# The odd layer's S5 and MLA half rewritten: regrouping through DRAM, scans in pieces, the mask as four extra contraction rows, weight loads issued ahead

## The chip, the cores and the metric

The kernel runs on one core of a Trainium2 chip. The metric is device time in microseconds (us), the median of several executions. Engines are named as the profile names them: PE is TensorE (matmul), DVE is VectorE, ACT is ScalarE, POOL is GpSimd, SP is SyncE, which here only issues DMAs.

## The reference, cut to what matters

A trunk of two residual layers over x (1, 512, 1024) in float32. Layer 0 (even) is Mamba-2 beside differential attention; layer 1 (odd) is an S5 complex-diagonal SSM beside multi-head latent attention (MLA). Each mixer is followed by a SwiGLU. The change lies in the odd mixer:

```python
u, c_q, c_kv, k_rope = split_cols(h @ w_in, ODD_SIZES)      # 512, 384, 256, 32 columns
# S5: 32 groups of 16 channels, a complex state of 64 per group
bu = einsum('bsgh,gph->bsgp', ug, b_bar)
state = associative_scan(s5_combine, (a_el, bu), axis=1)
y = real(einsum('bsgp,ghp->bsgh', state, cm)) + d_skip * ug
y = gelu(y);  y_c = y * sigmoid(y @ w_glu + b_glu)
# MLA, 8 heads, key chunk of 64 <= query chunk of 64
q = rms_norm(c_q, q_norm) @ w_uq;  kv = rms_norm(c_kv, kv_norm) @ w_ukv
p = softmax(where(mask, (qn @ kn.T + qr @ k_rot.T) * scale, -inf));  y_d = p @ v
out = concatenate([y_c, y_d]) @ w_out
```

## The kernel before, in words

Activations stand feature-major, as 128 x 512 tiles (features on partitions, time on columns). A projection is a list of **units**. A unit is one output block of 128 columns; it is computed by `mm3` (L178 to L180) in three passes per k-tile, high by high, low by high and high by low, because weights and activations are split into two float32r halves. 24 matmuls of 128 x 512 make a unit with eight k-tiles. `prep` loads a chunk of weights (`wload`, L157, two buffers `raw`) and splits one unit of it: ACT casts the high half (`whi`, L169), DVE subtracts the low half (`wlo`, L170). There are two buffers of each half, two PSUM buffers `mm` for the results of units, and two each of `sc`, `tp` and `po`.

`drive` walks one hand-written list of units and closures, and prepares the next unit ahead of computing one. `later(n, f)` puts a closure off by n units. A scheduler then keeps each engine's instructions nearly in that order; every engine works through its own queue in order, and waits on semaphores.

In the odd layer the list is: four units of u; two of ck (256 columns of the latent key and value); three of cq (384 of the latent query); kr (32 rotary key columns); then the value product, the first query and key units of MLA, the GLU, the attention. Four S5 steps Q = 0 to 3 (128 channels each) lie between the units:

- `ev_u` scales u and regroups it into `u4[Q]` with 16 copies of 32 x 128, half on DVE and half on ACT (L1262).
- `s5a` makes 8 products u by b of 128 columns in two `sc` buffers (L1273), turns them by four multiplies on DVE (L1281 to L1284) and two sums on POOL, scans with eight `tensor_tensor_scan` (L1289), and turns back (L1299 to L1304) into `hr` and `hi`.
- `s5b`, two units later, makes 12 products (L1312 to L1315), adds the skip (L1320), takes the GELU on ACT, and regroups into `yf[Q]` with 16 more copies (L1326).

`ev_c` reads a unit of ck or cq out of its `mm` buffer three times: ACT high half, DVE low half (L344), ACT square (L273, L276). POOL sums the squares (L281), and `rows_k` and `rows_q` make the norms from a small PE product of that sum (L309) and a chain of 4-column DVE instructions. `attend`, `flip` and `scores` run the MLA heads in 16 steps (four pairs of heads by four query blocks). A score (L1412) is a product over 96 rows (64 plain and 32 rotary) in plain float32; a bfloat16 product of one row (L1414, `mrow` by `nrow`) adds -1e30 on the last 64 keys for the first 64 queries. The second head's probabilities are scaled on POOL (L1420).

Of the kernel before, what the change touches and what calls it, by code (L numbers as in the profile page):

```python
# [14 lines left out]
ALU = mybir.AluOpType  # L15
# [106 lines left out]
class Trunk:  # L122
# [81 lines left out]

# [39 lines left out]
    def drive(self, items):  # L244
        us = [x for x in items if isinstance(x, dict)]
        nxt = {id(u): v for u, v in zip(us, us[1:])}
        self.prep(us[0])
        for x in items:
            if isinstance(x, dict):
                if id(x) in nxt:  # L250
                    self.prep(nxt[id(x)])
                self.compute(x)
            else:
                x()
# [14 lines left out]
    def stat_add(self, st, src, pool=None, tag="sacc"):  # L269
# [4 lines left out]
        else:  # L274
            sq = self.t(self.tmp, [P, T], "sq")
            nc.scalar.activation(out=sq, in_=src, func=AF.Square)  # L276
            self.padd(st["acc"], st["acc"], sq)

# [91 lines left out]
    def setup(self):  # L370
# [12 lines left out]
        self.raws, self.kept = {}, {}  # L383
# [848 lines left out]
    def odd(self, E):  # L1232
# [7 lines left out]
        def start():  # L1240
            nonlocal sp
            sp = self.pool(ctx, "od")
            self.norm_done(E)
# [11 lines left out]
        def ev_u(Q, ps):  # L1255
# [4 lines left out]
            for q in range(4):  # L1260
                for i in range(4):
                    (A.copy if i % 2 else V.tensor_copy)(out=u4[Q][32 * i:32 * i + 32, q, :],  # L1262
                                                         in_=us[32 * q:32 * q + 32, i * P:(i + 1) * P])
# [4 lines left out]
        def s5a(Q):  # L1268
            S = self.s5
            pb = [self.ps("sc") for _ in range(2)]  # L1270
# [15 lines left out]
            self.padd(t[2], t[2], t[3], ALU.subtract)  # L1286
            for q in range(4):
# [4 lines left out]
            c_, s_ = (S[n][Q].rearrange("p q c -> p (q c)") for n in ("rc", "rs"))  # L1292
            if Q % 2:
                hr, hi = (t5(f"b{ri}{Q // 2}").rearrange("p (q c) -> p q c", q=4) for ri in range(2))
# [10 lines left out]
            self.later(2, lambda: s5b(Q, hr, hi))  # L1305

        def s5b(Q, hr, hi):
            S = self.s5
# [15 lines left out]
            for j in range(4):  # L1324
                for q in range(4):
                    (A.copy if q % 2 else V.tensor_copy)(out=yf[Q][32 * q:32 * q + 32, j * P:(j + 1) * P],  # L1326
                                                         in_=yy[32 * j:32 * j + 32, q * P:(q + 1) * P])
# [62 lines left out]
        def ev_qk(m, n):  # L1390
            def f_(ps):
                if n == 0:
                    qk[m] = [None, None]
                x = qk[m][n] = [t5(f"{('b1', 'rc')[n]}{2 * (m % 2) + hh}") for hh in range(2)]
# [11 lines left out]
        def scores(m, qb):  # L1406
# [3 lines left out]
            for hh in range(2):  # L1410
                ps = self.ps("sc")
                PE.matmul(ps[:, :n], lhsT=qk[m][0][hh][0:96, qb * P:(qb + 1) * P], rhs=qk[m][1][hh][0:96, :n],  # L1412
                          start=True, stop=False)
                PE.matmul(ps[:, n - 64:n], lhsT=self.mrow, rhs=self.nrow, start=False, stop=True)  # L1414
# [4 lines left out]
            for hh, e in enumerate((V, G)):  # L1419
                e.tensor_scalar(out=pp[hh][:, :n], in0=pp[hh][:, :n], scalar1=rr[:, hh:hh + 1], scalar2=None,  # L1420
                                op0=ALU.mult)
# [218 lines left out]
```

## Time and profile before

| what | value |
|---|---|
| median of 3 runs | 1457.12 us (1453.04 to 1458.03) |
| the profiled execution | 1457.81 us |
| its span, first to last instruction | 1456.0 us |
| PE busy over the span | 1395.0 us (96%) |
| DVE, ACT, POOL busy | 950.5, 674.0, 257.3 us |
| mean granted PE clock | 0.985 |

The span is what the trace covers; 1.8 us of the execution lie outside it. A busy share is the time in which an engine had an instruction running. The odd layer's first unit ends near 839 us of the span and its last near 1084.

### The profile page before, as it was taken

Reading aid. Unit: us, or ns where it says so; the run is one execution under the profiler, and the core shown is the slowest. Engines: PE = TensorE matmul, PEld = TensorE weight load, DVE = VectorE, ACT = ScalarE, POOL = GpSimd, SP = SyncE. Lnnn points to the kernel's source line nnn. Section 1 sums busy time; section 2 is a strip of 40 time slices with the busy share of each in tenths; the row PEclk is TensorE's granted clock in tenths of the full one; section 3 lists DMA queues with packets and bytes.
Section 4 is the critical chain, followed back from the end, with each engine's and each line's share of the span. In section 5 each row is a group of like instructions: output and inputs, shape, how many; then the busy total and the mean of one; then the engine's idle time right before and its main releaser. Section 6 shows DMA issues by size and latency. Waiting matters only on the chain.

```text
span 1456.0 us, 18392 instructions
## 1 busy us (share of the span) xinstructions
PE 1395.0 (96%) x6979; PEld 1142.9 (78%) x6979; DVE 950.5 (65%) x1992; ACT 674.0 (46%) x1222; POOL 257.3 (18%) x208
## 2 busy tenths in 40 slices
PE   8999989999999999999999987789999999999997
PEld 5877878888888777888888876666788888888887
DVE  6988788878766998773644589676664433433453
ACT  6658777867643443333232443365453322322342
POOL 0234511000012110010011313413121100100111
PEclk9999999999999999999999998889999999999999
DMA  5211121222213222222323211110222322223231
GB/s 183 81 72 59 59 87 44 73 73 73 88 58 116 75 90 104 96 88 83 112 88 104 89 55 36 54 47 1 87 87 93 111 87 95 105 80 111 87 102 59
DMA packets 20280, 119.83 MB, mean 82 GB/s; under 512 B 2384, under 2 KB 3024, under 8 KB 9056
## 3 DMA queue, kind: packets, MB, share of 16 engines
q1 hardware_dynamic: 18896, 116.89, 23.2%
q10 hardware_dynamic: 1296, 1.76, 0.4%
q8 instruction: 55, 0.90, 0.3%
q14 instruction: 33, 0.27, 0.1%
HBM read 116.55 MB, written 2.10 MB: 81 GB/s over the span
## 4 chain that ended last, share of the span: by engine, by line
PE 69%; DVE 20%; ACT 6%; issue 2%; POOL 2%; DMA 1%; SPq 0%; ACTq 0%; DVEq 0%; POOLq 0%
PE mm L178 13%; PE mm L179 13%; PE mm L180 13%; PE sc L180 7%; PE sc L179 7%; PE sc L178 7%; DVE wlo L170 3%; DVE qsw L608 2%; ACT qsw L768 1%; PE sc L1412 1%; ACT whi L169 1%; POOL xs L281 1%; PE po L1440 1%; PE po L857 1%; PE tp L1430 1%
## 5 line engine op out<-in xcount | busy, mean ns | idle before, releaser
L169 ACT CAST whi<-raw 128x1024 fp32r<-128x1024 f32 (+5 forms) x231 | 224.1, 970 | 537.9 <-PE mm L179 306.8
L170 DVE TENSOR_TENSOR wlo<-raw,whi 128x1024 fp32r<-128x1024 f32 (+5 forms) x231 | 264.9, 1147 | 43.8 <-ACT whi L169 28.9
L281 POOL TENSOR_TENSOR gt<-gt,rbc 128x512 f32<-128x512 f32 x44 | 76.3, 1736 | 572.7 <-ACT gt L967 572.7
L972 DVE TENSOR_TENSOR gt<-mm,gt 128x512 f32<-128x512 f32 x44 | 30.4, 690 | 110.9 <-PE mm L180 107.5
L281 POOL TENSOR_TENSOR sacc<-sacc,sq 128x512 f32<-128x512 f32 x29 | 45.2, 1558 | 262.8 <-issue 193.9
L966 DVE TENSOR_TENSOR gt<-sc,rbc 128x512 f32<-128x512 f32 x44 | 30.3, 689 | 89.1 <-PE sc L180 89.1
L180 PE MATMUL mm<-x0h,wlo 128*128 128x512 f32 (+2 forms) x91 | 36.9, 406 | 12.8 <-DVE wlo L170 12.8
L178 PE MATMUL mm<-x0h,whi 128*128 128x512 f32 (+2 forms) x91 | 38.9, 428 | 8.2 <-ACT x0h L343 6.0
L987 DVE TENSOR_TENSOR h<-h,mm 128x512 f32<-128x512 f32 x20 | 13.7, 687 | 44.0 <-PE mm L180 44.0
L768 ACT ACTIVATE qsw<-mm 32x512 f32<-32x512 f32 x64 | 37.7, 590 | 6.5 <-DVE qraw L764 5.7
L987 DVE TENSOR_TENSOR h<-h,sc 128x512 f32<-128x512 f32 x20 | 13.7, 686 | 38.8 <-PE sc L180 38.8
L967 ACT ACTIVATE gt<-gt 128x512 f32<-128x512 f32 x44 | 27.6, 628 | 22.9 <-DVE gt L966 22.9
L180 PE MATMUL mm<-x1h,wlo 128*128 128x512 f32 (+2 forms) x91 | 37.2, 409 | 0.0
L179 PE MATMUL mm<-x2l,whi 128*128 128x512 f32 (+2 forms) x91 | 37.1, 407 | 0.0
L178 PE MATMUL mm<-x7h,whi 128*128 128x512 f32 (+2 forms) x95 | 37.1, 390 | 0.0
L180 PE MATMUL mm<-x7h,wlo 128*128 128x512 f32 (+2 forms) x95 | 37.1, 390 | 0.0
L179 PE MATMUL mm<-x7l,whi 128*128 128x512 f32 (+2 forms) x95 | 37.0, 389 | 0.0
L178 PE MATMUL mm<-x1h,whi 128*128 128x512 f32 (+2 forms) x91 | 36.5, 401 | 0.3 <-ACT x1h L343 0.3
L179 PE MATMUL mm<-x0l,whi 128*128 128x512 f32 (+2 forms) x91 | 36.6, 402 | 0.2 <-DVE x0l L344 0.2
L178 PE MATMUL mm<-x2h,whi 128*128 128x512 f32 (+2 forms) x91 | 36.7, 404 | 0.0
L180 PE MATMUL mm<-x2h,wlo 128*128 128x512 f32 (+2 forms) x91 | 36.7, 403 | 0.0
L179 PE MATMUL mm<-x1l,whi 128*128 128x512 f32 (+2 forms) x91 | 36.4, 400 | 0.2 <-DVE x1l L344 0.2
(939 smaller groups left out, 4366.3 us busy)
## 6 DMA issues: line engine op xcount, KB each, us to landing
raw<-in_f_dram SPq DMA_DIRECT2D x52, 1024.0 KB, 4.8
raw<-in_w_dram SPq DMA_DIRECT2D x35, 1024.0 KB, 4.9
raw<-in_f_dram SPq DMA_DIRECT2D x16, 896.0 KB, 4.5
raw<-in_w_dram SPq DMA_DIRECT2D x8, 512.0 KB, 3.6
h<-in_xt_dram SPq DMA_DIRECT2D x8, 256.0 KB, 5.9
raw<-in_w_dram SPq DMA_DIRECT2D x2, 640.0 KB, 4.0
out_dram<-otm SPq DMA_DIRECT2D x4, 256.0 KB, 2.5
out_dram<-otm ACTq DMA_DIRECT2D x4, 256.0 KB, 2.8
```

The source lines that it names most:

```text
L169: nc.scalar.copy(out=hi[:, :n], in_=raw[:, o:o + n])
L170: nc.vector.tensor_tensor(out=lo[:, :n], in0=raw[:, o:o + n], in1=hi[:, :n].bitcast(F32), op=ALU.subtract)
L178: nc.tensor.matmul(ps, lhsT=hi[:, k, :m], rhs=xh, start=start and j == 0, stop=False)
L179: nc.tensor.matmul(ps, lhsT=hi[:, k, :m], rhs=xl, start=False, stop=False)
L180: nc.tensor.matmul(ps, lhsT=lo[:, k, :m], rhs=xh, start=False, stop=stop and j == n - 1)
L281: self.nc.gpsimd.tensor_tensor(out=out, in0=x, in1=y, op=op)
L608: V.scalar_tensor_tensor(out=acc, in0=xr[:, 1 + k:1 + k + T], scalar=self.par("cw", 12 * k + j), in1=acc, op0=ALU.mult, op1=ALU.add)
L768: A.activation(out=sw[c * 32:(c + 1) * 32, :], in_=ps[d * 32:(d + 1) * 32, :], func=AF.Identity, scale=scale)
L966: V.tensor_tensor(out=gt, in0=ps, in1=E["rbc"], op=ALU.mult)
L967: A.activation(out=gt, in_=gt, func=AF.Silu)
L972: V.tensor_tensor(out=gt, in0=ps, in1=gt, op=ALU.mult)
L987: V.tensor_tensor(out=self.h[i], in0=self.h[i], in1=ps, op=ALU.add)
```

## The change

- **Regrouping.** `regroup` replaces the 32 copies of an S5 step (16 for u4, 16 for yf): one DMA writes the 128 x 512 tile to DRAM, four DMAs read it back, 32 partitions each, all issued on SP.
- **Pieces.** `s5a` and `s5b` become one generator with three `yield`s; the list calls the pieces at chosen places. The products go to `po` buffers instead of `sc`.
- **Mask.** Four rows of the input `cmask` are loaded by DMA (issued on ACT) into rows 96 to 99 of the query and key tiles, eight DMAs of 4 x 512. A score is one product over 100 rows; the 32 one-row products go. Head pairs 2 and 3 use the tiles of pairs 0 and 1 again.
- **Scaling.** The second head's probabilities are scaled on ACT instead of POOL.
- **Loads.** `fetch` issues the next chunk's weight DMA as soon as fewer than two loaded chunks still have units to split. On SP this only changes what stands ahead of what: the load before the other DMAs.

```diff
+    def fetch(self):
+        for k in self.order:
+            if k not in self.raws:
+                if sum(self.left[x] > 0 for x in self.raws) >= 2:
+                    return
+                self.raws[k] = self.wload(k)
...
+    def regroup(self, out, src):
+        d = self.t(self.dram, [P, T], "regroup", bufs=4)
+        self.nc.sync.dma_start(out=d, in_=src)
+        for i in range(4):
+            self.nc.sync.dma_start(out=out[32 * i:32 * i + 32],
+                                   in_=d.rearrange("(q p) (i c) -> p i q c", q=4, i=4)[:, i])
...
-            for q in range(4):
-                for i in range(4):
-                    (A.copy if i % 2 else V.tensor_copy)(out=u4[Q][32 * i:32 * i + 32, q, :],
-                                                         in_=us[32 * q:32 * q + 32, i * P:(i + 1) * P])
+            self.regroup(u4[Q], us)
...
-            pb = [self.ps("sc") for _ in range(2)]
+            pb = [self.ps("po") for _ in range(2)]
...
-            self.later(2, lambda: s5b(Q, hr, hi))
-
-        def s5b(Q, hr, hi):
-            S = self.s5
+            yield
...
-                x = qk[m][n] = [t5(f"{('b1', 'rc')[n]}{2 * (m % 2) + hh}") for hh in range(2)]
+                if m < 2:
+                    x = [t5(f"{('b1', 'rc')[n]}{2 * (m % 2) + hh}") for hh in range(2)]
+                    for hh in range(2):
+                        A.dma_start(out=x[hh][96:100, :], in_=a["cmask"][4 * n:4 * n + 4, :])
+                else:
+                    x = qk[m - 2][n]
+                qk[m][n] = x
...
-                PE.matmul(ps[:, :n], lhsT=qk[m][0][hh][0:96, qb * P:(qb + 1) * P], rhs=qk[m][1][hh][0:96, :n],
-                          start=True, stop=False)
-                PE.matmul(ps[:, n - 64:n], lhsT=self.mrow, rhs=self.nrow, start=False, stop=True)
+                PE.matmul(ps[:, :n], lhsT=qk[m][0][hh][0:100, qb * P:(qb + 1) * P],
+                          rhs=qk[m][1][hh][0:100, :n], start=True, stop=True)
...
-            for hh, e in enumerate((V, G)):
-                e.tensor_scalar(out=pp[hh][:, :n], in0=pp[hh][:, :n], scalar1=rr[:, hh:hh + 1], scalar2=None,
-                                op0=ALU.mult)
+            V.tensor_scalar(out=pp[0][:, :n], in0=pp[0][:, :n], scalar1=rr[:, 0:1], scalar2=None, op0=ALU.mult)
+            A.mul(out=pp[1][:, :n], in_=pp[1][:, :n], mul=rr[:, 1:2])
...
-        items = [start] + uu
-        items += [L(s5a, 0), uck[0], L(s5a, 1), uck[1], lambda: self.later(1, rows_k, rows_k2), ucq[0], L(s5a, 2),
-                  ucq[1], ucq[2], L(s5a, 3), lambda: self.later(1, rows_q, rows_q2)] + ukr
-        items += [uv, uqr(0)] + uqk(0) + uqk(1) + [uqr(1)]
+        items = [start] + uu[:3] + [s5(0), uu[3], s5(0), uck[0], s5(1, 0), uck[1], lambda: self.later(1, rows_k, rows_k2),
+                                    s5(1), ucq[0], s5(1), s5(0), ucq[1], s5(2), ucq[2], s5(2, 1),
+                                    lambda: self.later(1, rows_q, rows_q2)]
+        items += ukr + [s5(3, 2), uv, s5(3, 2), uqr(0), s5(3)] + uqk(0) + [s5(3)] + uqk(1) + [uqr(1)]
```

What the order of instructions becomes, at three places.

**The first S5 step, DVE and PE.** DVE before, from the copies of the last u unit on (t and hr, hi belong to step Q = 0; raw_7825 holds the weights of ck, and wlo_7914 is the low half of ck's second unit):

```order
L1262 COPY u_1457_7858<-us_7856 32x128 x8
L1281 TENSOR_TENSOR t_1460_7885<-sc_7875,rc_1134_5482 128x512
L1282 TENSOR_TENSOR t_1461_7886<-sc_7876,rs_1135_5483 128x512
L1283 TENSOR_TENSOR t_1462_7887<-sc_7876,rc_1134_5482 128x512
L1284 TENSOR_TENSOR t_1463_7888<-sc_7875,rs_1135_5483 128x512
L1289 SCALAR_TENSOR_TENSOR t_1460_7885<-s5r_1065_4973,t_1460_7885 128x128 x4
L1289 SCALAR_TENSOR_TENSOR t_1462_7887<-s5r_1065_4973,t_1462_7887 128x128 x4
L1299 TENSOR_TENSOR hr_7903<-t_1460_7885,rc_1134_5482 128x4x127
L1301 TENSOR_TENSOR hi_7904<-t_1462_7887,rc_1134_5482 128x4x127
L1303 TENSOR_TENSOR hr_7903<-hr_7903,t_1461_7886 128x4x127
L170 TENSOR_TENSOR wlo_7914<-raw_7825,whi_7913 128x1024
L344 SCALAR_TENSOR_TENSOR ck0l_7943<-mm_7917,par_94,ck0h_7942 128x512
```

DVE now, at the same place (wlo_7868 is the low half of ck's second unit, wlo_7935 that of cq's first):

```order
L170 TENSOR_TENSOR wlo_7868<-raw_7658,whi_7867 128x1024
L1304 TENSOR_TENSOR t_1459_7811<-po_7801,rc_1135_5484 128x512
L1307 TENSOR_TENSOR t_1462_7814<-po_7801,rs_1136_5485 128x512
L1305 TENSOR_TENSOR t_1460_7812<-po_7802,rs_1136_5485 128x512
L1306 TENSOR_TENSOR t_1461_7813<-po_7802,rc_1135_5484 128x512
L1313 SCALAR_TENSOR_TENSOR t_1459_7811<-s5r_1066_4975,t_1459_7811 128x128 x4
L1313 SCALAR_TENSOR_TENSOR t_1461_7813<-s5r_1066_4975,t_1461_7813 128x128 x4
L1325 TENSOR_TENSOR hr_7924<-t_1459_7811,rc_1135_5484 128x4x127
L1327 TENSOR_TENSOR hi_7925<-t_1461_7813,rc_1135_5484 128x4x127
L1329 TENSOR_TENSOR hr_7924<-hr_7924,t_1460_7812 128x4x127
L170 TENSOR_TENSOR wlo_7935<-raw_7765,whi_7934 128x1024
L368 SCALAR_TENSOR_TENSOR ck0l_7899<-mm_7873,par_94,ck0h_7898 128x512
```

The copies are gone, and each split has moved up by one unit: ck's second stands ahead of step 0 and cq's first behind it. PE before, from the end of step 0's second products (mm_8064 is cq's first unit, sc_8095 step 1's second products, tp_8131 the sum of ck's squares):

```order
L1315 MATMUL sc_8024<-hi_7904,cx_1097_5157 128x128
L178 MATMUL mm_8064<-x0h_7393,whi_7988 128x512
...
L180 MATMUL mm_8064<-x7h_7638,wlo_7989 128x512
L1312 MATMUL sc_8095<-u_1446_7760,tt_1160_5723 128x128
...
L309 MATMUL tp_8131<-ones_97,sacc_7946 128x1 x4
L1273 MATMUL sc_8156<-u_1451_7808,b_1193_6033 128x128 x4
```

PE now (mm_7938 is ck's second unit, mm_7984 cq's first, mm_8080 cq's second; sc_8050 is step 0's second products):

```order
L180 MATMUL mm_7938<-x7h_7640,wlo_7868 128x512
L178 MATMUL mm_7984<-x0h_7397,whi_7934 128x512
...
L180 MATMUL mm_7984<-x7h_7640,wlo_7935 128x512
L333 MATMUL tp_8015<-ones_97,sacc_7902 128x1 x4
L1335 MATMUL sc_8050<-u_1445_7745,tt_1124_5397 128x128
...
L178 MATMUL mm_8080<-x0h_7397,whi_7978 128x512
```

The sum of ck's squares (tp) now stands ahead of step 0's second products, which stood one unit before it.

**SP, from the last u units on.** Before, these are weight loads alone. Now (regroup is the DRAM tile, us the scaled u or the S5 output, u the regrouped u4, and raw_8194 of before is raw_7871 here):

```order
L157 DMA raw_7765<-in_w_dram 128x2048
L298 DMA regroup_7746<-us_7743 128x512
L298 DMA regroup_7755<-us_7752 128x512
L300 DMA u_1445_7745<-regroup_7746 32x4x128 x4
L300 DMA u_1448_7754<-regroup_7755 32x4x128 x4
L298 DMA regroup_7795<-us_7792 128x512
L298 DMA regroup_7853<-us_7850 128x512
L157 DMA raw_7871<-in_w_dram 128x1280
L300 DMA u_1455_7794<-regroup_7795 32x4x128 x4
L300 DMA u_1467_7852<-regroup_7853 32x4x128 x4
L157 DMA raw_7982<-in_w_dram 128x1408
L298 DMA regroup_8070<-us_8063 128x512
```

Two writes stand ahead of the reads of the first, and one weight load stands between the third and fourth write and their reads.

**ACT, where the GLU meets the first attention steps.** Before, the sigmoid of the last GLU unit and the exponentials of the first scores (us is the sigmoid's output, rs the probabilities):

```order
L1457 ACTIVATE us_8725<-mm_8712,par_94 128x512
L1416 ACT_TABLE_LOAD
L1416 ACTIVATE rs_1639_8735,ssum_8733<-sc_8737,nmx_8732 128x512
L1462 CAST t_1634_8728<-us_8725 128x512
L1416 ACTIVATE rs_1640_8736,ssum_8733<-sc_8742,nmx_8732 128x512
L169 CAST whi_8925<-raw_8923 128x512
```

Now, from the third GLU unit's sigmoid on:

```order
L1481 ACTIVATE us_8633<-mm_8620,par_94 128x512
L1441 ACT_TABLE_LOAD
L1441 ACTIVATE rs_1655_8683,ssum_8681<-sc_8685,nmx_8680 128x384
L1486 CAST t_1637_8636<-us_8633 128x512
L1481 ACT_TABLE_LOAD
L1481 ACTIVATE us_8657<-mm_8644,par_94 128x512
L1441 ACT_TABLE_LOAD
L1441 ACTIVATE rs_1656_8684,ssum_8681<-sc_8689,nmx_8680 128x384
L1486 CAST t_1643_8660<-us_8657 128x512
```

Sigmoids and exponentials alternate now. Over the whole program ACT loads a function table 31 times instead of 28; all three are in this stretch.

## Rows read from the trace of the kernel before

**Rows 1.** Windows: length, busy us of PE, PEld, DVE, ACT, POOL, PE clock, DMA.

```profile
860.00:885.00 25.00, 16.35 (x84) 13.50 (x82) 24.59 (x33) 4.33 (x7) 14.16 (x14) 0.86 0.09 27
885.00:910.00 25.00, 19.69 (x103) 16.83 (x104) 21.84 (x58) 11.11 (x25) 7.17 (x6) 0.86 0.08 29
910.00:942.00 32.00, 25.35 (x130) 19.47 (x129) 24.31 (x53) 11.87 (x24) 16.57 (x10) 0.93 0.18 60
942.00:962.00 20.00, 15.67 (x63) 13.15 (x64) 13.29 (x29) 10.43 (x24) 2.63 (x2) 0.69 0.00 1
1000.00:1057.00 57.00, 57.00 (x338) 39.30 (x337) 33.03 (x76) 25.62 (x68) 13.11 (x11) 1.00 0.16 56
```

**Rows 2.** PE's waits between 830 and 1090: total us, times, longest.

```profile
PE mm L180 <- DVE wlo L170: 12.2, 3, 6.1
PE tp L326 <- DVE rkr L319: 4.8, 1, 4.8
PE sc L1312 <- ACT b L1379: 4.4, 1, 4.4
PE mm L178 <- DVE b L1397: 3.5, 1, 3.5
```

**Rows 3.** Timeline of DVE in the S5 stretch: start, us, instruction.

```profile
847.03 1.06 DVE L1257 TENSOR_TENSOR us<-sc,rbc 128x512 f32<-128x512 f32 x1
...
870.11 2.27 DVE L170 TENSOR_TENSOR wlo<-raw,whi 128x1024 fp32r<-128x1024 f32 x1
872.30 0.74 DVE L344 SCALAR_TENSOR_TENSOR ck0l<-mm,par,ck0h 128x512 fp32r<-128x512 f32 x1
...
885.39 0.74 DVE L344 SCALAR_TENSOR_TENSOR ck1l<-mm,par,ck1h 128x512 fp32r<-128x512 f32 x1
```

**Rows 4.** Timeline of ACT, 870 to 980.

```profile
873.13 0.60 ACT L273 ACTIVATE sacc<-mm 128x512 f32<-128x512 f32 x1 [7.60 <-DVE ck0l L344]
...
886.16 0.60 ACT L276 ACTIVATE sq<-mm 128x512 f32<-128x512 f32 x1 [5.32 <-DVE ck1l L344]
...
968.21 1.28 ACT L1457 ACT_TABLE_LOAD   x1
969.51 0.69 ACT L1457 ACTIVATE us<-mm,par 128x512 f32<-128x512 f32 x1
```

**Rows 5.** Timeline of POOL, the sum of ck's squares.

```profile
886.83 1.28 POOL L281 TENSOR_TENSOR sacc<-sacc,sq 128x512 f32<-128x512 f32 x1 [2.37 <-ACT sq L276]
```

**Rows 6.** Timeline of PE: ck's second unit, then scores without and with the mask product.

```profile
865.59 0.48 PE L178 MATMUL mm<-x0h,whi 128*128 128x512 f32 x1
...
961.95 1.02 PE L1412 MATMUL sc<-rc,b 96*128 96x512 f32 x2
...
963.04 0.40 PE L179 MATMUL mm<-cq0l,whi 128*128 128x512 f32 x1
963.27 0.39 PE L180 MATMUL mm<-cq0h,wlo 128*128 128x512 f32 x1
...
991.69 1.12 PE L1412 MATMUL sc<-rc,b 96*128 96x512 f32 x2
992.74 0.20 PE L1414 MATMUL sc<-nrow,mrow 1*128 1x64 bf16 x1
992.87 1.12 PE L1412 MATMUL sc<-rc,b 96*128 96x512 f32 x2
```

**Rows 7.** Groups of instructions, 836 to 1060: count, busy us, mean ns.

```profile
L1416 ACT ACTIVATE rs<-sc,nmx 128x512 f32<-128x512 f32 (+3 forms) x32 | 16.9, 528 | 16.2 <-DVE nmx L1415 14.8 <-DVE rsum L1418 1.0
...
L1326 DVE COPY yf<-us 32x128 f32<-32x128 f32 x32 | 7.9, 248 | 0.4
```

**Rows 8.** Page, DMA issues: count, KB each, median us from issue to landing.

```profile
raw<-in_w_dram SPq DMA_DIRECT2D x35, 1024.0 KB, 4.9
...
h<-in_xt_dram SPq DMA_DIRECT2D x8, 256.0 KB, 5.9
...
out_dram<-otm SPq DMA_DIRECT2D x4, 256.0 KB, 2.5
```

**Rows 9.** The line of the weight loads between 836 and 1090: ns to issue one.

```profile
L157 SPq DMA_DIRECT2D raw<-in_w_dram x10: 327/328/328, 847.1 to 1047.6; - x10
```

More of the change, by code (lines that the diff above doesn't have):

```diff
@@ L200, in prep @@
         o = sum(CH[u["key"]][2][:u["sub"]])
+        self.left[u["key"]] -= 1
         u["w"] = self.wsplit(self.raws[u["key"]], o, u["nk"], u["m"], u["keep"])
@@ L246, in drive @@
         nxt = {id(u): v for u, v in zip(us, us[1:])}
+        seen = set()
+        for u in us:
+            if u["keep"] is None or u["keep"] not in seen:
+                self.left[u["key"]] = self.left.get(u["key"], 0) + 1
+            seen.add(u["keep"])
+        self.order = list(self.left)
         self.prep(us[0])
@@ L251, in drive @@
                     self.prep(nxt[id(x)])
+                self.fetch()
                 self.compute(x)
@@ L382, in setup @@
         self.n_unit = 0
-        self.raws, self.kept = {}, {}
+        self.raws, self.kept, self.left = {}, {}, {}
         self.queue, self.held = [], None
@@ L1242, in start @@
             sp = self.pool(ctx, "od")
+            self.dram = self.pool(ctx, "swap", space=bass.MemoryType.DRAM)
             self.norm_done(E)
@@ L1291, in s5a @@
                                          x[:, q * P:(q + 1) * P], 0.0, op0=ALU.mult, op1=ALU.add)
-            c_, s_ = (S[n][Q].rearrange("p q c -> p (q c)") for n in ("rc", "rs"))
-            if Q % 2:
-                hr, hi = (t5(f"b{ri}{Q // 2}").rearrange("p (q c) -> p q c", q=4) for ri in range(2))
+            yield
+            if Q == 1:
+                hr, hi = (t5(f"b{ri}0").rearrange("p (q c) -> p q c", q=4) for ri in range(2))
+            elif Q == 3:
+                hr, hi = (t2(f"t{ri}", shape=[P, 4, P]) for ri in range(2))
             else:
@@ L1304, in s5a @@
             G.tensor_tensor(out=hi[:, :, 1:P], in0=hi[:, :, 1:P], in1=v4(t[3]), op=ALU.add)
-            self.later(2, lambda: s5b(Q, hr, hi))
-        def s5b(Q, hr, hi):
-            S = self.s5
+            yield
             ps = self.ps("sc")
@@ L1323, in s5b @@
             yf[Q] = t2(f"yf{Q}")
[L1324 to L1327, printed above, removed]
+            self.regroup(yf[Q].rearrange("p (j c) -> p j c", j=4), yy)
         cq, ck = [None] * 3, [None] * 2
@@ L1489, in odd, with s5, f_ @@
         uv = self.unit("vq", 0, None, None, body=values)
-        items = [start] + uu
-        items += [L(s5a, 0), uck[0], L(s5a, 1), uck[1], lambda: self.later(1, rows_k, rows_k2), ucq[0], L(s5a, 2),
-                  ucq[1], ucq[2], L(s5a, 3), lambda: self.later(1, rows_q, rows_q2)] + ukr
-        items += [uv, uqr(0)] + uqk(0) + uqk(1) + [uqr(1)]
+        gens = {}
+        def s5(*Qs):
+            def f_():
+                for Q in Qs:
+                    if Q not in gens:
+                        gens[Q] = s5a(Q)
+                    next(gens[Q], None)
+            return f_
+        items = [start] + uu[:3] + [s5(0), uu[3], s5(0), uck[0], s5(1, 0), uck[1], lambda: self.later(1, rows_k, rows_k2),
+                                    s5(1), ucq[0], s5(1), s5(0), ucq[1], s5(2), ucq[2], s5(2, 1),
+                                    lambda: self.later(1, rows_q, rows_q2)]
+        items += ukr + [s5(3, 2), uv, s5(3, 2), uqr(0), s5(3)] + uqk(0) + [s5(3)] + uqk(1) + [uqr(1)]
         steps = [(m, qb) for m in range(4) for qb in (3, 2, 1, 0)]
```

## Prediction

> **What bounds the kernel now.** I looked first at the busy shares, where TensorE has 96% of the span, and then at the stretches in which it has less. The windows show four of them, one after the other, from 860 to 962 us: TensorE is busy 16.35 of 25, 19.69 of 25, 25.35 of 32 and 15.67 of 20 us, and the granted clock is 0.86, 0.86, 0.93 and 0.69 [rows 1]. That is the S5 stretch. The reader is to see two losses there. TensorE is idle for 8.65 + 5.31 + 6.65 + 4.33 = 24.9 us. What it does run, it runs slower: busy time times the missing clock is 16.35 x 0.14 + 19.69 x 0.14 + 25.35 x 0.07 + 15.67 x 0.31 = 11.7 us. Together 36.6 us is the most that any new order of this stretch can give. Later, from 1000 to 1057, TensorE is busy all the time at full clock [rows 1]; only work taken off it counts there.
>
> The list of TensorE's waits then says for whom it waits: 12.2 us in three waits for the low halves of weights, which DVE splits, and 4.8, 4.4 and 3.5 us for other results of DVE and ACT [rows 2]. These six sum to 24.9, so the list is complete. In the first window DVE is busy for 24.59 of 25 us [rows 1]: it goes through the turns and scans of one S5 step (10 us) before it reaches the split that TensorE waits for.
>
> **The change, by its parts.** The sum is made against the profiled execution, 1457.81 us with a span of 1456.0; the median of the three runs is 0.7 below it.
>
> *The first wait goes.* Everything ahead of ck's second unit on TensorE stays the same work, so that unit begins at 865.6 as before [rows 6]. Its split now stands ahead of step 0's DVE work, so the wait of 6.1 us is gone [rows 2]. Its 24 matmuls at 0.23 us, the distance of two starts [rows 6], end at 871.1.
>
> *A smaller one comes.* cq's first unit needs an `mm` buffer, and there are two: ck's first must have been read three times. DVE does its part (ck0l) behind the split at 870.11, and ends at 873.0 [rows 3]; the ACT square ends at 873.7 [rows 4]. TensorE waits 873.7 - 871.1 = 2.6 us. The unit then ends at 879.2, or some 1 us later at a lower clock.
>
> *The largest wait is then the sum of ck's squares.* In the new order it stands behind cq's first unit and ahead of step 0's second products. It needs POOL's sum, which needs ACT's square, which needs ck1l on DVE, and DVE still has step 1's turns and scans ahead of that. Ck1l began at 885.39 [rows 3], the square at 886.16 [rows 4], the sum ended at 886.83 + 1.28 = 888.1 [rows 5]. No copy lay ahead of them on DVE but those of u, which end before step 0 begins in both, so I take the same times: TensorE stands still from about 880 to 888, 8 us.
>
> *The rest of the stretch.* DVE loses the yf copies, 7.9 us [rows 7], which lay between its later splits; TensorE's chain from here on follows DVE. Walking the new order with the durations of these rows, I find a wait of under 1 us for the sum of cq's squares, and two of about 2 us around step 2's second products (for the last POOL sum of that step, and for the small DVE chain of cq's norm, now interleaved with step 3's scans). Where 3.0 + 4.4 + 3.5 = 11 us of waits stood in the last 35 us before [rows 2], I count 4.6.
>
> Idle in all: 2.6 + 8 + 0.6 + 4 = 15 us, between 11 (the last ones vanish) and 20 (they stay). For the clock I take 6 us instead of 11.7: six waits cost about 2 us each, and three or four remain. Sum for the stretch: 36.6 - 15 - 6 = 15.6 us gained, with bounds of 9 (20 idle, 7.5 clock) and 22 (11 idle, 3.5 clock).
>
> *The mask products.* A score and its mask follow one another at 992.87 - 991.69 = 1.18 us. A score of the same size without a mask behind it took, with one matmul of 0.23, 963.04 - 961.95 = 1.09 us, so 0.86 alone [rows 6]. The difference is 0.32 us, times 32 is 10.2. By the distance from a mask to the next score, 992.87 - 992.74 = 0.13 [rows 6], it is 4.2. I take 8.5, nearer to the first, since that is the whole distance; the 100 rows in place of 96 cost nothing that I can see, as a matmul's time here goes by its 512 columns. All of it counts, since TensorE is never idle there [rows 1].
>
> *ACT gets more.* Sixteen scalings at about 0.5 us (an exponential of the same shapes takes 0.53 [rows 7]) are 8 us. In the steady part ACT is busy 25.62 of 57 us [rows 1], so they hide. Eight issues of mask rows at 0.33 us, the price on SP [rows 9], hide too. But at the start of the attention ACT alternates between sigmoid and exponential, three table loads more at 1.28 us each; after the load at 968.21 the sigmoid starts at 969.51, so a load costs 1.30 [rows 4]. The fourth score's exponential stands behind two loads, two sigmoids and a cast there, and the next score needs its buffer. I count 2.5 us of wait for TensorE and 1 of clock: 3.5 lost, between 0 and 6. The Trainium skill, ScalarE: Activation LUTs, section "What ACT_TABLE_LOAD costs", has a drain of about 1.38 us beside each load, 2.66 us a switch; by that three loads cost 8.0 us instead of 3.9, and the predicted time would be 4 us longer. The trace shows no such gap behind the load.
>
> *The trips through DRAM.* One trip is an issue (0.33), a write of 256 KB (2.5), four issues (1.3) and the last read, which I bound by another 2.5: 6.7 us [rows 8, 9]. The first u tile is scaled at 848.1 [rows 3], so u4 is there at 855, or at 857 if the 1 MB load just ahead of it (4.9 us [rows 8]) holds it up. TensorE reaches it at 865.6 less 19 matmuls (4.3) and two sets of eight products, 857.9 (a product of 128 columns at a quarter of 0.86, so 1.7 a set). The later trips have more room; the tightest is the last yf, with 2 us to spare. Cost: 0. If each leg took the 5.9 us of the input loads [rows 8], the trip is 13.4 us, and these two come 4 us late each.
>
> *Loads.* The weights were always loaded well ahead: the list of TensorE's waits has no DMA in it [rows 2]. The order of the weight loads among themselves stays. Worth 0.
>
> Sum: 15.6 + 8.5 - 3.5 = 20.6 us. 1457.8 - 20.6 = 1437.2; less the 0.7, **1436**.
>
> **The rivals.** *Late trips:* the DRAM legs take 5.9 us, u4 and yf come 4 us late each, and each delay costs another 1.5 of clock: 11 us less gain, 1447. For it speaks that these writes queue behind weight loads; against it, the 2.5 us of the output writes. The Trainium skill, DMA: Bandwidth & Descriptors, section "Anatomy of one DMA", says that the completion of a write to HBM can take surprisingly long; the row of the output writes, also to DRAM, has a median of 2.5.
>
> *More than I count:* the waits around step 2 vanish and the mask gives its 10.2: 22 + 10.2 - 1 = 31 gained, 1426.
>
> *It does nothing:* the 8 us wait grows to what the old ones were, since DVE's chain of turns and scans is still whole and still feeds TensorE; the stretch gains 0, the mask 4.2, the tables cost 4: 1457. Against it: the 7.9 us of copies were in that chain.
>
> *Slower, by the clock:* TensorE runs in bursts of 5 us between waits for DVE. If the clock stays at 1.2 GHz for the whole way from 871 to 943, some 50 us of work at 2.4 GHz take 50 more instead of the 6 I counted. The verdict turns when about 27 us of that work run at half clock (6 counted + 20.6 gain), and with 36 it ends at 1466. The worst window of before, 0.69 [rows 1], lasted 20 us.
>
> **Chances.** My forecast, 14 to 27 us gained, 0.58; late trips 0.16; more than counted 0.11; nothing 0.06; slower 0.09. The range takes in the first, the late trips and half of the third: 1424 to 1450; the forecast's own is 1430 to 1443. A difference of 0.3% (4.4 us) is about what a measurement of this kernel can tell from none. Faster: 0.58 + 0.16 + 0.11 = 0.85; same 0.06; slower 0.09.
>
> **What would show it.** In the new trace ck's second unit has no wait inside it; the longest wait of TensorE before the attention is at the small product of ck's squares, near 888, for POOL; the first score starts about 16 us earlier than 961.95; no wait of TensorE is for a DMA; a score of 512 keys takes 0.86 us from start to next start; and near the GLU TensorE waits for an exponential. I am wrong if the products of step 0 wait for u4, if the clock is lower than before over the S5 stretch, or if in the attention TensorE waits for ACT at every step.

## The result and the profile after

The changed kernel takes 1439.55 us, the median of 4 runs (1437.43 to 1440.54), against 1457.38 of before on the same chip (4 runs, 1453.04 to 1458.03). The ratio is 0.9882, with a 95% interval of 0.986 to 0.9904. That is 17.8 us less by the medians and 17.2 by the ratio. The prediction was 1436 (20.6 us less), and its own range 1430 to 1443. The profiled execution took 1439.68 us, its span is 1437.8 us and the mean granted clock 0.987.

From the odd layer on, line numbers after are 20 to 30 higher than before. The windows of the S5 stretch and of the start of the attention, against [rows 1] (columns as there):

```profile
860.00:885.00 25.00, 20.77 (x99) 16.88 (x98) 23.30 (x33) 3.75 (x5) 13.17 (x12) 0.93 0.25 75
885.00:910.00 25.00, 21.67 (x120) 19.76 (x121) 15.15 (x37) 8.44 (x12) 8.22 (x7) 0.86 0.26 85
910.00:942.00 32.00, 28.69 (x150) 22.59 (x149) 27.81 (x58) 10.21 (x18) 17.70 (x15) 0.89 0.18 62
942.00:962.00 20.00, 18.47 (x85) 14.01 (x84) 17.55 (x33) 13.55 (x23) 3.52 (x3) 1.00 0.22 70
962.00:1000.00 38.00, 35.39 (x197) 25.16 (x196) 25.92 (x56) 33.41 (x73) 0.00 (x0) 0.91 0.08 28
```

TensorE's idle time from 860 to 962 is 4.23 + 3.33 + 3.31 + 1.53 = 12.4 us, where it was 24.9, and the clock takes 20.77 x 0.07 + 21.67 x 0.14 + 28.69 x 0.11 = 7.6 us, where it took 11.7. New is the loss from 962 to 1000: 2.6 us idle and 35.39 x 0.09 = 3.2 us of clock. The same window before had 37.23 us busy at full clock:

```profile
962.00:1000.00 38.00, 37.23 (x184) 24.44 (x182) 29.73 (x56) 25.74 (x52) 10.25 (x7) 1.00 0.13 45
```

TensorE's longest waits from 830 to 1090, against [rows 2]:

```profile
PE tp L333 <- POOL sacc L305: 5.5, 1, 5.5
PE sc L1438 <- ACT rs L1441: 2.2, 2, 1.6
PE mm L178 <- ACT sacc L289: 2.1, 1, 2.1
PE tp L350 <- DVE rqr L343: 1.8, 1, 1.8
PE mm L178 <- ACT us L1481: 1.3, 1, 1.3
PE sc L1338 <- POOL hi L1330: 1.0, 1, 1.0
```

The three waits for `wlo` are gone. TensorE's timeline at the places which the prediction named, in brackets the idle time before an instruction and what ended it, against [rows 6]:

```profile
839.68 0.95 PE L333 MATMUL tp<-ones,sacc 128*128 128x1 f32 x8
...
859.78 2.02 PE L1296 MATMUL po<-u,b 128*128 128x128 f32 x16 [0.65 <-issue]
...
867.70 0.48 PE L178 MATMUL mm<-x0h,whi 128*128 128x512 f32 x1
...
875.49 0.50 PE L178 MATMUL mm<-x0h,whi 128*128 128x512 f32 x1 [2.09 <-ACT sacc L289]
...
888.33 1.87 PE L333 MATMUL tp<-ones,sacc 128*128 128x1 f32 x8 [5.46 <-POOL sacc L305]
...
890.62 0.63 PE L1336 MATMUL sc<-hr,cx 128*128 128x128 f32 x2
...
894.46 0.39 PE L1338 MATMUL sc<-hi,cx 128*128 128x128 f32 x2
...
947.00 1.02 PE L1438 MATMUL sc<-rc,b 100*128 100x512 f32 x2
...
1016.14 1.98 PE L1438 MATMUL sc<-rc,b 100*128 100x512 f32 x4
1017.97 0.39 PE L1454 MATMUL tp<-cst,rs 128*128 128x128 f32 x2
```

ck's second unit (867.70) has no wait inside. The longest wait is at 888.33, for POOL's sum of ck's squares. Behind it the small products run at half speed: a group of two spans 0.63 us at 890.62, and 0.39 us at 894.46, where the clock is back. The first score starts at 947.00, where it started at 961.95. In the steady part two scores take 1017.97 - 1016.14 = 1.83 us, where two scores with their masks took 2 x 1.18 = 2.36.

TensorE's timeline at the odd layer's start, and the scores by their line (count, ns of one, first and last start), both before:

```profile
838.49 0.95 PE L309 MATMUL tp<-ones,sacc 128*128 128x1 f32 x8
```

```profile
L1412 PE MATMUL sc<-rc,b x64: 275/483/697, 961.9 to 1048.1; 96*128 96x512 f32 x16, 96*128 96x384 f32 x16, 96*128 96x256 f32 x16, 96*128 96x128 f32 x16
```

and the scores after:

```profile
L1438 PE MATMUL sc<-rc,b x64: 274/484/697, 947.0 to 1030.3; 100*128 100x512 f32 x16, 100*128 100x384 f32 x16, 100*128 100x256 f32 x16, 100*128 100x128 f32 x16
```

The account of the 18.2 us between the two spans: the odd layer's first small product came at 838.49 before and at 839.68 now, 1.2 lost before the odd layer begins (the last section has the likely place). From there to the first score: 123.46 before, 107.32 now, 16.1 gained. First to last score: 86.2 before (961.9 to 1048.1) and 83.3 now (947.0 to 1030.3), 2.9 gained. The remaining 0.4 lies behind.

### The profile page after: what moved, and what is told of

It is laid out like the page before. It is cut to its first block, busy times and chain, and to the rows that moved or that the text cites. A ratio compares the mean times of both kernels' runs of the same rounds, so it can differ in the third digit from the quotient of the medians.

```text
span 1437.8 us, 18260 instructions
## 1 busy us (share of the span) xinstructions
PE 1387.4 (96%) x6947; PEld 1144.3 (80%) x6947; DVE 932.4 (65%) x1928; ACT 665.0 (46%) x1177; POOL 235.7 (16%) x192
## 3 DMA queue, kind: packets, MB, share of 16 engines
q10 hardware_dynamic: 1360, 1.83, 0.4%
## 4 chain that ended last, share of the span: by engine, by line
PE 74%; DVE 15%; ACT 5%; issue 2%; POOL 2%; DMA 1%; SPq 0%; ACTq 0%; DVEq 0%; POOLq 0%
PE mm L178 14%; PE mm L179 14%; PE mm L180 14%; PE sc L180 7%; PE sc L179 7%; PE sc L178 7%; DVE wlo L170 2%; PE sc L1438 1%; ACT qsw L792 1%; POOL xs L305 1%; ACT whi L169 1%; DVE qsw L632 1%; PE po L1464 1%; PE po L881 1%; PE mm L776 1%
## 5 line engine op out<-in xcount | busy, mean ns | idle before, releaser
L179 PE MATMUL mm<-x3l,whi 128*128 128x512 f32 (+2 forms) x91 | 36.2, 397 | 0.3 <-DVE x3l L365 0.3
```

Of the source, the lines that this page charges most:

```text
L179: nc.tensor.matmul(ps, lhsT=hi[:, k, :m], rhs=xl, start=False, stop=False)
```

## The experiments

The theory to be tested: the S5 stretch gives 15.6 us by order and trips together, the mask 8.5, the alternating tables take back 3.5, the early loads are nothing. Every ratio below is to the kernel before, run on the same chip beside it, whose medians were 1458.40 us for e1 to e4, 1457.64 for e5 to e8, 1456.98 for e9 to e11 and 1456.90 for e12.

| run | median us | ratio, 95% interval |
|---|---|---|
| e1_mask_only | 1449.26 | 0.9944 (0.9930 to 0.9957) |
| e2_copies_back | 1448.41 | 0.9939 (0.9926 to 0.9952) |
| e3_trips_only | 1448.64 | 0.9933 (0.9918 to 0.9948) |
| e4_no_fetch | 1438.82 | 0.9872 (0.9857 to 0.9887) |
| e5_pool_scale | 1439.01 | 0.9870 (0.9855 to 0.9885) |
| e6_sig_first | 1440.34 | 0.9881 (0.9868 to 0.9894) |
| e7_mask_trips | 1444.58 | 0.9910 (0.9892 to 0.9927) |
| e8_sum_later | 1430.64 | 0.9817 (0.9805 to 0.9829) |
| e9_order_only | 1452.04 | 0.9963 (0.9950 to 0.9976) |
| e10_no_mask | 1445.45 | 0.9917 (0.9903 to 0.9931) |
| e11_later_tags | 1432.19 | 0.9831 (0.9818 to 0.9845) |
| e12_fill | 1433.71 | 0.9840 (0.9826 to 0.9855) |

The changed kernel did not run beside these. Where a difference from it is given below, it is one of medians; by the ratios it comes out up to 1.2 us differently.

### One part alone

**The mask (e1).** The kernel before with the change's two hunks on `x` and on the score:

```diff
...
-                PE.matmul(ps[:, :n], lhsT=qk[m][0][hh][0:96, qb * P:(qb + 1) * P], rhs=qk[m][1][hh][0:96, :n],
-                          start=True, stop=False)
-                PE.matmul(ps[:, n - 64:n], lhsT=self.mrow, rhs=self.nrow, start=False, stop=True)
+                PE.matmul(ps[:, :n], lhsT=qk[m][0][hh][0:100, qb * P:(qb + 1) * P],
+                          rhs=qk[m][1][hh][0:100, :n], start=True, stop=True)
```

> The kernel before with one part of the change: the mask as four more contraction rows, no product of one row behind each score. Everything else, the scaling on POOL and the copies too, is as before. Theory of the prediction: each of the 32 small products stood on TensorE's path with 0.27 us, so 8.5 us less than before, about 1449. Rival: only the 0.13 us between its start and the next score counts, 4.2 us less, 1453. Second rival: the attention follows DVE and ACT, nothing changes, 1457.

Measured: 1449.26, 9.1 us less by the medians, 8.2 by the ratio. The theory's 8.5 holds; 4.2 is outside the interval.

**The trips (e3).** The kernel before with both sets of copies replaced:

```diff
-            for q in range(4):
... (16 copies)
+            self.regroup(u4[Q], us)
...
-            for j in range(4):
... (16 copies)
+            self.regroup(yf[Q].rearrange("p (j c) -> p j c", j=4), yy)
```

> The kernel before with one part of the change: the five DMAs through DRAM in place of the 32 copies per S5 step, in the old order of the S5 work. Theory: the copies lay in DVE's chain, which TensorE follows, but the splits still stand behind ten microseconds of turns and scans each, so only the copies' own time comes off: 5 to 8 us less than before, about 1451. Rival one: nothing, since in the old order the DMA's results come as late as the copies' did, 1457. Rival two: the order of the pieces was not needed, 14 us less, 1443.

Measured: 9.8 us less by medians and by ratio, above the theory's 5 to 8, and less than the 14 of rival two. Its list of TensorE's waits up to 965:

```profile
PE sc L1378 <- ACT b L1382: 6.0, 1, 6.0
...
PE mm L180 <- DVE wlo L170: 1.7, 2, 1.4
```

Even in the old order the three waits for `wlo` shrink from 12.2 to 1.7 us, so the copies in front of the splits did more to them than I had thought; the longest wait is now one for ACT. From 860 to 962 TensorE's idle time falls from 24.9 to 18.6 us and what the clock takes from 11.7 to 5.1: the theory had counted only time that DVE gets back, and half of what the trips gave in this stretch is clock.

**The order (e9).** The changed kernel with copies, mask product and POOL's scaling of before; only the order and the early loads are left.

```diff
-            self.regroup(u4[Q], us)
+            for q in range(4):
... (16 copies; 16 more in place of the regroup of yf, and the hunks of e10 and e5)
```

> The changed kernel with only the order of the S5 pieces and the early loads left of the change: copies on DVE and ACT, the mask as a product of one row, scaling on POOL. Theory: with the copies in it, DVE's chain is as long as before, and the new order only decides in front of which product TensorE waits; with the copies back the changed kernel still gained 10 us, the mask rows make 5 to 9 of these, so 1 to 5 us less than before, 1455. Rival one: the order is worth its 6 us even with the copies, 1451 or less. Rival two: without the trips the order is a loss, 1460.

Measured: 1452.04, 4.9 us less by the medians, 5.4 by the ratio (3.5 to 7.3). The theory put 1455 and a gain of 1 to 5, rival one 6 or more: the result lies between them, and the interval holds both. The order is a gain by itself. It comes here with the pieces, the `po` buffers, the early loads and the alternating tables, which no run separates from it but for the loads (e4) and the tables (e6). The wait list has other waits in place of most of those for `wlo`:

```profile
PE tp L333 <- POOL sacc L305: 7.1, 1, 7.1
PE sc L1338 <- ACT b L1405: 4.0, 1, 4.0
```

### One part taken out

**Copies back (e2).** The changed kernel with the 32 copies per step in place of `regroup`:

```diff
-            self.regroup(u4[Q], us)
+            for q in range(4):
... (16 copies, DVE and ACT in turn; the same for yf)
```

> The changed kernel, but with the 32 copies per S5 step on DVE and ACT in place of the five DMAs; pieces, mask, scaling and loads stay as changed. Theory: with the new order DVE still feeds TensorE in the S5 stretch, so the 7.9 us of copies of the S5 outputs on DVE come back into its chain, and those of u partly: 6 to 10 us more than the changed kernel, about 1448. Rival one: the order of the pieces alone made the gain, the copies fit into DVE's gaps: within 2 us of the changed kernel, 1440. Rival two: the trips through DRAM made all of the gain in the S5 stretch, about 15 us more, 1455.

Measured: 1448.41, 8.9 above the changed kernel (8.3 by the ratios), the size that the theory had. Its reason holds only in part. TensorE waits 2.7 us for DVE's low halves again, but more for ACT, which does half of the copies: 2.6 us for high halves and 3.6 for ACT's reading of the value product (L1405; 0.4 in the changed kernel, L1399).

**No early loads (e4).**

```diff
-                self.fetch()
```

> The changed kernel without the early issue of the weight loads: each load is issued where the unit ahead of its first use is prepared. Theory: worth nothing, within 1.5 us of the changed kernel, 1440, and no wait of TensorE for a DMA. Rival: the writes and reads of the trips now stand ahead of loads on SP's queue, each of which waits for its source, so loads come late: 3 to 8 us more, 1443 to 1448, with waits for the high halves of weights in the S5 stretch.

Measured: 1438.82, which is 0.7 below the changed kernel (1.5 by the ratios) and less than the intervals can tell. No wait of TensorE from 830 to 1000 is for a DMA. Worth nothing, as predicted.

**Scaling on POOL (e5).**

```diff
-            A.mul(out=pp[1][:, :n], in_=pp[1][:, :n], mul=rr[:, 1:2])
+            G.tensor_scalar(out=pp[1][:, :n], in0=pp[1][:, :n], scalar1=rr[:, 1:2], scalar2=None, op0=ALU.mult)
```

> The changed kernel with the second head's probabilities scaled on POOL again. Theory: ACT is full at the start of the attention because of function tables, not of the scalings, and in the steady part it has room, so within 1.5 us of the changed kernel, 1440. Rival: the sixteen scalings of 0.56 us fill ACT where TensorE waits for it, so 2 to 4 us less, 1437.

Measured: 1439.01, 0.5 below the changed kernel. Nothing, as the theory had it, but not for its reason alone: from 942 to 1000 TensorE's waits for exponentials (2.2 us) are gone, and 2.1 us of waits for POOL's scalings stand in their place. The trace reads as if the scalings cost TensorE about as much there on either engine.

**No mask rows (e10).** The changed kernel with the mask product of before.

```diff
... (the hunk on x as before, the score over 96 rows)
-                          rhs=qk[m][1][hh][0:100, :n], start=True, stop=True)
...
+                          start=True, stop=False)
+                PE.matmul(ps[:, n - 64:n], lhsT=self.mrow, rhs=self.nrow, start=False, stop=True)
```

> The changed kernel with the mask as a product of one row again; order, trips, scaling and loads as changed. Theory: the S5 stretch by itself gives the 15.6 us of the prediction, and the alternating tables cost 1 to 4, so 12 to 15 us less than before, 1443.5, and the mask rows are worth only some 4 to 5 in this kernel, as they were on top of the trips in the old order. Rival: the mask rows are worth their 9 us here too, 1448.5.

Measured: 1445.45, 11.5 less than before by the medians, 12.1 by the ratio. This is the S5 term with the tables, 15.6 - 3.5 = 12.1 in the prediction. So in the changed kernel the mask is worth 5 to 6 us (17.2 - 12.1 by the ratios, 1445.45 - 1439.55 by the medians).

**Mask and trips in the old order (e7).** The edits of e1 and e3 together.

> The kernel before with two parts of the change, the mask rows and the trips through DRAM, in the old order of the S5 work, scaling on POOL, no early loads. Alone, the mask gave 9.1 us and the trips 9.8 us against the same runs of before. Theory one, the two add up and the new order's gain is eaten by the alternating tables: about 1439, the same as the changed kernel within 2 us. Theory two, the order of the pieces is worth some us net: 1442 to 1445.

Measured: 1444.58 (1440.70 to 1449.14), 13.1 less. Theory two. On top of the trips the mask gives 3.3 (ratios) to 4.1 us (medians), not 9.1: TensorE is idle for 38 - 34.20 = 3.8 us of the window from 962 to 1000,

```profile
962.00:1000.00 38.00, 34.20 (x189) 22.33 (x188) 28.48 (x61) 30.62 (x66) 9.38 (x9) 1.00 0.08 28
```

where before it had 0.8. The waits there are for POOL's scalings (1.3 us), for ACT's high halves (1.1) and exponentials (1.0): my reading is that TensorE, with less work of its own, gets to where these aren't ready.

### What the waits cost

**Tables (e6).** The changed kernel, with an edge of order on ACT:

```diff
+                if m == 0 and qb == 3:
+                    self.tc.add_manual_dep(e.ins, W["sig", 3].ins.name, ...)   # exponential behind the last sigmoid
```

> The changed kernel with one edge of order on ACT: the first exponential of the attention stands behind the last GLU sigmoid, so that ACT loads its tables 28 times again and not 31. Theory: the alternation costs TensorE 3 to 4 us of waits and 3 us of clock around 955 to 980, most of which comes back: 3 to 6 us less than the changed kernel, 1435. Rival: the scores wait for the sigmoids then, and TensorE has as much to wait for as before, or more: within 1.5 us, 1440.

Measured: 1440.34. The rival. The windows from 945 to 962 and 962 to 1000, and TensorE's waits:

```profile
945.00:962.00 17.00, 14.08 (x53) 10.22 (x52) 12.91 (x24) 8.93 (x14) 2.95 (x2) 0.91 0.21 71
962.00:1000.00 38.00, 36.50 (x212) 25.40 (x211) 28.10 (x63) 31.68 (x75) 0.00 (x0) 1.00 0.08 28
```

```profile
PE mm L178 <- ACT us L1485: 2.0, 1, 2.0
...
PE sc L1438 <- ACT rs L1441: 0.5, 2, 0.3
```

The wait for exponentials shrinks from 2.2 to 0.5 us, but that for the sigmoid grows from 1.3 to 2.0, and two for DVE come to 1.9 where there was one of 0.3. From 942 to 1000 the waits sum to 4.4 us, in the changed kernel to 4.2. The window from 945 to 962 has 2.9 us idle (1.5 in the changed kernel), and the clock falls there, 0.91 for 1.00, and not from 962 to 1000. My reading is that TensorE has too little else to do at this place, whatever ACT does first.

**The sum one unit later (e8).**

```diff
-... lambda: self.later(1, rows_k, rows_k2) ...
+... lambda: self.later(2, rows_k, rows_k2) ...
```

> The changed kernel with the small product of ck's squares one unit later, behind cq's second unit, so that step 0's second products stand ahead of it. Theory: TensorE's longest wait, 5.5 us near 888 for POOL, shrinks to about 1 to 2 us, since the second products run in it and cq's second unit then waits only for the square of ck's second unit near 886.8: 3 to 5 us less, 1436. Rival: the wait moves to the next thing that DVE or ACT is late with, and nothing changes, 1440.

Measured: 1430.64, 8.9 below the changed kernel and 27 below before: the best of all that ran, more than the theory's 3 to 5 and more than the wait of 5.5 us that it was to remove. The waits up to 945, and the windows:

```profile
PE tp L350 <- DVE rqr L343: 4.5, 1, 4.5
PE mm L178 <- ACT sacc L289: 2.1, 1, 2.1
PE mm L178 <- ACT sq L292: 1.3, 1, 1.3
```

```profile
860.00:885.00 25.00, 22.64 (x117) 18.99 (x115) 23.79 (x33) 3.76 (x5) 13.94 (x12) 0.93 0.23 71
885.00:910.00 25.00, 23.46 (x132) 18.45 (x132) 20.64 (x46) 10.18 (x16) 10.70 (x11) 1.00 0.25 86
910.00:942.00 32.00, 27.48 (x151) 23.74 (x151) 31.02 (x63) 13.03 (x24) 14.66 (x11) 0.95 0.25 82
...
962.00:1000.00 38.00, 35.63 (x228) 25.39 (x228) 27.90 (x65) 30.96 (x77) 0.00 (x0) 1.00 0.08 28
```

With the window from 942 to 962 (18.16 us busy at full clock) the idle time from 860 to 962 is 10.3 us (12.4 in the changed kernel), but the clock takes 3.0 in place of 7.6. From the odd layer's first product to the first score it is 939.4 - 839.4 = 100.0 us, 7.3 less than in the changed kernel. The clock takes nothing from 962 to 1000 either, where it took 3.2; but it is 1.00 there in e5, e6 and e10 too, which keep the wait, so that this comes from the later sum isn't shown.

**ck in other buffers (e11).** e8, and ck's units in the `sc` buffers, so that cq's need not wait until ck's are read:

```diff
-        uck = self.units("ck", 2, xs8, ev_c(ck, "ck", sk_, "kn"))
+        uck = self.units("ck", 2, xs8, ev_c(ck, "ck", sk_, "kn"), tags=("sc",))
```

> The changed kernel with the product of ck's squares one unit later, as in the run before this one, and ck's two units in the other pair of PSUM buffers, so that cq's units no longer wait until ck's are read. Theory: the waits of 2.1 and 1.3 us for ACT go, 2 to 4 us less than with the later product alone, 1428. Rival: TensorE only comes sooner to what DVE hasn't split yet, the same as with the later product alone, 1430.5 within 1.5 us.

Measured: 1432.19, 1.7 more than e8 (2.0 by the ratios), where the rival allowed 1.5: no gain, and the theory's 2 to 4 us are out. Both waits for ACT are gone, and waits for DVE's splits are back:

```profile
PE mm L180 <- DVE wlo L170: 3.8, 3, 3.0
```

**TensorE kept busy (e12).** The changed kernel, and in `rows_k` ahead of the sum:

```diff
+            for j in range(24):
+                f = PE.matmul(fill, lhsT=hi[:, j % 8, :], rhs=xs[j % 8][0], start=j == 0, stop=j == 23)
... (and an edge of order that keeps the first of them behind cq's first unit)
```

> The changed kernel with 24 more matmuls of 128 x 512, whose result nobody reads, between cq's first unit and the small product of ck's squares: 5.5 us at 0.23 each, just the wait that stands there. What the kernel computes is the same. The small product still has to wait for POOL until about 888.3. Theory: a wait costs its own time and then again in clock; with TensorE kept busy the work behind it runs at 2.4 GHz, and of the 3 to 6 us that the clock took from the S5 stretch 2 to 5 come back: 1436. Rival: only the wait's own time counts, and what runs faster behind it waits for DVE all the same: within 1.5 us of the changed kernel, 1440. Second rival: the 24 matmuls run at half clock, end behind POOL, and cost up to 5 us, 1445.

Measured: 1433.71 (1432.16 to 1436.88), 5.8 us less than the changed kernel takes, with 24 matmuls more; the theory had 2 to 5. The mean granted clock of its runs is 0.990 to 0.993, that of the changed kernel's 0.985 to 0.988. TensorE's timeline at the wait, and the windows:

```profile
888.52 0.39 PE L1379 MATMUL tp<-x7h,whi 128*128 128x512 f32 x1
890.65 1.05 PE L333 MATMUL tp<-ones,sacc 128*128 128x1 f32 x8 [1.74 <-POOL sacc L305]
...
891.87 0.39 PE L1336 MATMUL sc<-hr,cx 128*128 128x128 f32 x2
```

```profile
860.00:885.00 25.00, 22.07 (x113) 18.24 (x112) 23.01 (x33) 4.67 (x6) 11.62 (x11) 1.00 0.30 87
885.00:910.00 25.00, 23.26 (x141) 20.34 (x140) 17.96 (x39) 8.43 (x12) 9.98 (x9) 1.00 0.26 85
```

The last of the 24 starts at 888.52, and the sum still waits for POOL, 1.74 us. It starts 48.9 us behind the odd layer's first product, as in the changed kernel (48.65), so nothing of the waiting for POOL was removed. What changed is the clock behind it: from 885 to 910 it is 1.00, where it is 0.80 to 0.86 in the changed kernel and in e2, e4, e5, e6, e9 and e10, which all keep the wait. Two small products behind the wait span 0.39 us at 891.87 and not 0.63. (The 1.00 from 860 to 885 can't be put down to the 24 matmuls, which start only at 883.31; e5 has it without them.) From the sum to the first score it is 946.5 - 890.65 = 55.9 us in place of 947.00 - 888.33 = 58.7, and 58.6 to 59.3 in e4, e5, e6 and e10; e12's other waits in between are those of the changed kernel within 0.1 us. So 2.8 us or a little more are what the clock behind this wait takes. Another 2.4 lie between the first and the last score (80.9 us for 83.3), where the clock is 1.00 from 962 to 1000 and was 0.91 in the changed kernel; e5, e6 and e10 have 1.00 there with the wait in place, so that this comes from the same wait isn't shown.

## Why the prediction was right, point by point

- **The first wait goes:** right. The unit starts 2.1 us later than in [rows 6], 1.2 of them lost ahead of the odd layer and 0.65 at u4.
- **A smaller one comes, 2.6 us:** 2.09, for the ACT square (875.49). Right.
- **The largest is the sum of ck's squares, 8 us near 888:** 5.46 at 888.33, for POOL; cq's first unit came later and partly at half clock (its matmuls start 0.43 us apart from 877.0 to 880.0, and not 0.23), which ate into it. In e2, e4, e5, e6 and e9 the wait is 7.1. Right in place and cause, somewhat long in size.
- **The rest of the stretch, 4.6 us:** the waits at L350, L1338 and L1335 are 1.8 + 1.0 + 0.4 = 3.2. The clock took 7.6 and not 6. The idle time from 860 to 962 was 12.4 and not 15. The stretch as a whole gained 16.1, against 15.6: this is closer than its two parts, because one error offset most of the other, and that is luck.
- **The mask, 8.5 us:** right by itself (8.2 to 9.1 in e1; 1.83 us for two scores in place of 2.36, 0.27 each, times 32 is 8.5). A score took 0.915 us from start to next start and not 0.86; the 8.5 stood between two readings and was a choice. Wrong was that "all of it counts, since TensorE is never idle there": this was read from the windows of before, and in the changed kernel TensorE is idle 2.6 us from 962 to 1000, and slower. There the mask is worth 5 to 6 (e10). The step that failed is this term of the sum: it was sized against a kernel without the other parts. By their ratios mask, trips and order alone give 8.2 + 9.8 + 5.4 = 23.4 us; together they give 17.2.
- **The tables, 3.5 us:** the alternation is there, and TensorE's waits are in the predicted place, 2.2 us. Its price is not shown: three loads fewer (e6) change nothing that can be told, since another wait takes the place. Of the drain beside a table load that the Trainium skill, ScalarE: Activation LUTs, section "What ACT_TABLE_LOAD costs", names, the trace of after shows none:

```profile
967.70 1.28 ACT L1481 ACT_TABLE_LOAD   x1
969.00 0.69 ACT L1481 ACTIVATE us<-mm,par 128x512 f32<-128x512 f32 x1
969.70 1.28 ACT L1441 ACT_TABLE_LOAD   x1
```

The load takes 1.28 us, the sigmoid starts 1.30 us after the load's start, and the next load right at the sigmoid's end.
- **Trips, 0 us:** nearly. u4 came at 859.78 and not at 855 to 857, and cost TensorE 0.65 us. The profile of after names nothing that ended this wait; e6 has it as `PE po L1296 <- DMA u<-regroup: 0.7, 1, 0.7`, and so have e5, e10 and e12, 0.7 to 0.9 us.

```profile
848.34 0.33 SPq L157 DMA_DIRECT2D raw<-in_w_dram  x1
849.37 1.23 SPq L298 DMA_DIRECT2D regroup<-us  x2
856.25 3.67 SPq L300 DMA_DIRECT2D u<-regroup  x8
```

The two writes are issued right behind a 1 MB load, and the first read only at 856.25, 6.9 us behind the first write; the eight reads take 0.46 us each to issue, not 0.33. The trace of after has no time to landing for these two writes; in e3, with the same load ahead of them, it is 6.2 and 5.9 us. The six later writes land in 2.1 to 2.2 us (2.0 to 2.1 in e3), somewhat sooner than the output writes [rows 8]. So the first trip took 859.78 - 849.37 = 10.4 us, between the 6.7 of the sum and the 13.4 of the rival: the rival was right about this write. The cost stayed at 0.65 us and not 8, since TensorE came to these products only at 859.1. The Trainium skill, DMA: Bandwidth & Descriptors, section "Anatomy of one DMA", says of DMAs on GpSimd's path that the completion of a write to HBM can take surprisingly long; these were issued on SP, and the slow ones are the two behind a load, so no run here shows that this was the reason.
- **Loads, 0 us:** right (e4).
- **The slower rival, the clock:** it did not decide, but it was the closest to something real. e12 shows 2.8 us of clock behind a single wait of 5.5; of the 5.8 in its median no more than that is traced to the wait.
- **The signs:** ck's second unit without a wait, the longest wait, the wait for an exponential near the GLU came as written; the first score came 15.0 us earlier, not 16. One failed in the small: TensorE does wait for a DMA, at u4, and by the letter "I am wrong if the products of step 0 wait for u4" came true, with 0.65 us. The clock is lower than before in one window (0.89 for 0.93 from 910 to 942), but over the stretch it takes 7.6 us and took 11.7.

What stays open: how much of e8's 8.9 us is the wait and how much the clock, since both moved; what the alternating tables cost; what the new order is worth without the `po` buffers; and whether the later waits at `rqr` (4.5 us in e8) can go too, which was not tried.

## What to carry to other kernels

Price a wait of TensorE twice, for its own length and for the clock behind it; where the wait couldn't go, even useless work put into it paid (e12, one place in one kernel). Price each part of a change against the kernel in which the other parts are already done: what is removed from an engine counts only while that engine is still the one that is waited for. And before moving big pieces of work, look at the small product in the list of waits: one digit, `later(2)` for `later(1)`, gave half as much as the whole change.

## What the runs showed that I had not expected

The clock differs between executions over instructions that are the same. e3 changes nothing in the even layer. Windows of 190 to 250, in that layer, before:

```profile
190.00:210.00 20.00, 18.95 (x98) 15.99 (x99) 18.68 (x44) 13.08 (x29) 2.58 (x2) 1.00 0.15 53
210.00:230.00 20.00, 15.53 (x68) 12.23 (x67) 19.32 (x29) 16.34 (x35) 5.11 (x4) 0.83 0.15 53
230.00:250.00 20.00, 18.02 (x138) 16.74 (x137) 16.13 (x45) 16.50 (x46) 3.06 (x2) 1.00 0.21 65
```

and in e3:

```profile
190.00:210.00 20.00, 19.35 (x89) 16.56 (x90) 16.49 (x40) 12.91 (x29) 1.32 (x2) 0.83 0.15 53
210.00:230.00 20.00, 15.83 (x67) 12.03 (x66) 19.34 (x28) 15.59 (x35) 6.37 (x5) 0.83 0.15 52
230.00:250.00 20.00, 17.66 (x134) 17.25 (x133) 15.38 (x45) 15.32 (x39) 3.14 (x2) 0.91 0.16 54
```

The loss is 15.53 x 0.17 = 2.6 us in the first and 19.35 x 0.17 + 15.83 x 0.17 + 17.66 x 0.09 = 7.6 us in the second. The profiled executions of e5 and e12 have the clock of the second. The changed kernel's has

```profile
190.00:210.00 20.00, 18.78 (x93) 16.08 (x94) 17.83 (x42) 13.07 (x29) 2.17 (x2) 0.91 0.15 53
```

and loses 18.78 x 0.09 = 1.7 us more there than before, which is the likely place of its 1.2 us ahead of the odd layer. Such a spread of 2 to 5 us is of the size of the smaller terms here, so a difference of two single traces over the whole span can't tell them; stretches between two marks of a trace, and medians, can.
